# A decoder trunk on one core: heads' results turned by transposing transfers of 16-bit planes, and one stream's low parts placed behind the second normalisation

## The chip, the core and the metric

The kernel runs on one core of one Trainium2 chip. The metric is the device time of one execution in microseconds (us). Three runs of the kernel before took 1221.09, 1221.14 and 1221.6 us; the median is 1221.14 us.

The engines are named as in the profile: PE is TensorE (matrix products), PEld its weight loads, DVE is VectorE, ACT is ScalarE, POOL is GpSimd, SP is SyncE, which here only issues transfers (DMAs).

## What is computed

A trunk of two layers over 256 tokens (T) of width 1024 (D). Each layer is a feed-forward block, a mixer and a second feed-forward block, with a layer normalisation behind each:

```python
for l in range(DEPTH):                       # DEPTH = 2, T = 256, D = 1024, D_FF = 2816
    h = _swiglu(x, ffn_w1[l, 0], ffn_w3[l, 0], ffn_w2[l, 0])
    x = _layernorm(ALPHA * x + 0.5 * h, ln_g[l, 0], ln_b[l, 0])
    h = _mixer(x, ...)
    x = _layernorm(ALPHA * x + h, ln_g[l, 1], ln_b[l, 1])
    h = _swiglu(x, ffn_w1[l, 1], ffn_w3[l, 1], ffn_w2[l, 1])
    x = _layernorm(ALPHA * x + 0.5 * h, ln_g[l, 2], ln_b[l, 2])

def _mixer(x, ...):
    u, v, q, k, val, gates = split(x @ w_in)
    h_a = _chunked_sgu(gelu(u), gelu(v), ...)          # position mixing in 128-token chunks
    o = _diff_attention(rope(q), rope(k), val, lam)    # 8 heads: softmax 1 - lam * softmax 2, times val
    h_b = _rmsnorm(o, diff_ln_g) * (1 - lam_init)      # per head, over its 128 values
    m = sigmoid(gate_A) * (h_a @ w_branch[0]) + sigmoid(gate_B) * (h_b @ w_branch[1])
    return m @ w_out
```

All of it is in float32.

## The kernel before, in words

**High and low parts.** Every large product is made of three: a float32 operand is cut into a high part that PE can multiply and a low part, the rest. For weights, ACT copies the high part (`whi`, L173, 128x1024 at a time) and DVE subtracts it from the raw weight (`wlo`, L177). `stream` loads 1 MB of weights into one of four `raw` buffers (a transfer on SP's queue) and cuts it so; eight `hi` and eight `lo` buffers of half a stream each hold the parts. A load waits until the low parts of the stream four places earlier are done. Where low parts stand among DVE's other work is steered by `behind(ins)`, which makes the scheduler issue an instruction after `ins` on its engine; `after` in `stream` names such an `ins` for a stream's low parts.

**The order of PE** is written out by hand. The long gemms call `beat(w)` as they go, which moves a clock of weights forward; side tasks (generators) are resumed at the beat they asked for with `yield`, and so the matmuls of attention stand between those of the projections. The other engines' order is set by a scheduler that follows priorities and `behind`.

**The mixer** first computes `val` (`gemm_b2`), then q and k for four pairs of heads (`rope`), then gates A and B (`gemm_a2` over `wa`, eight streams), then v, u and the two branches. `attend` runs beside this, once for a pair of heads (eight times in all): scores and their exponentials (L805, L815), transposes of the probabilities by PE (L839, L844) and their copies `aT` (L841, L846), products with `val` into a side bank (L852, L854), a copy of that bank to `on` (L857), the squares for the norm (L862, written back into the bank, with sums `ss`), a reciprocal root on POOL (`rsqrt4`), the scaling of `on` (L871), four transposes of `on` by PE into another side bank (L876), and from there the high and low parts of `hb` (L881 on ACT, L882 on DVE). There are four side banks (`sbank`) in PSUM, used in turn. `hb` is read by `branch(1, hb)`, behind the gates, v and u.

**The feed-forward block** already turns its results by transfers: `front` writes the two 16-bit halves of each float32 next to each other as planes (`planes`, L678, ACT), issues a transposing transfer on SP's queue (L680), and `columns` (L664, ACT) joins the halves again.

**Where two blocks meet**, the normalisation of the first (class `Norm`) works on two halves of the tokens, t = 0 and t = 1. `finish_s` for t = 1 makes the mean (`mv`), the sum of squares on ACT (L536), a chain of small DVE instructions for the reciprocal root (`ve`, `yi`, `nwa`, `nwy`, L227 to L233), and the scaled rows (`xtok`, L539, two halves; `norm.ends[1]` is the second of them). Then PE transposes them (L608), ACT scales them (`xf`, L614), and `x` is cut into high and low parts (L217, L218). Meanwhile `gemm_b2` of the next block works on t = 0. Its streams' parts are made ahead where `norm.pre` is set, which is where a feed-forward block ends and another block follows: three places in the program. In the others of the six normalisations `norm.pre` is not set.

Of the kernel before, what the change touches and what calls it, by code (L numbers as in the profile page):

```python
# [11 lines left out]
F32 = mybir.dt.float32  # L12
# [3 lines left out]
U16 = mybir.dt.uint16  # L16
AF = mybir.ActivationFunctionType
# [3 lines left out]
P = 128  # L21
D = 1024
T = 256
NT = T // P
# [8 lines left out]
SQ = [(FB + 2 * p, FB + 2 * p + 1) for p in range(NS)]  # L33
PQ = [(k, k + 1) for k in (0, 2, *range(FB + 2 * NS, FT, 2))]
HELD = 4
HEADS = 8
HD = 64
GROUPS = 8
# [19 lines left out]
def trunk(ctx, tc, x, xT, w13a, w13b, w2s, w2p, wb, wqk, wa, wbr, wo, gateb, sgug, sgub, sguwT, sgubias, lam, diffg,  # L58
          lng, lnb, lngT, lnbT, cosT, sinT, out):
    nc = tc.nc  # L60
    V, A, G, PE = nc.vector, nc.scalar, nc.gpsimd, nc.tensor
# [9 lines left out]
    tmp = ctx.enter_context(tc.tile_pool(name="tmp", bufs=2))  # L71
# [5 lines left out]
    def name(s):  # L77
        serial[0] += 1
        return f"{s}_{serial[0]}"

    def bank():
        return psum.tile([P, 512], F32, tag="main", name=name("bank"))

    def side_bank():
        return psum.tile([P, 512], F32, tag="side", name=name("sbank"))

    def slots(s, n, dtype=F32):

        return [act.tile([P, 512], dtype, tag="slot", name=name(s)) for _ in range((n + 1) // 2)]
# [22 lines left out]
    def step():  # L112
        chunk[0] += 1
        tc.cur_priority = chunk[0] * STEP
# [12 lines left out]
    def beat(w):  # L127

        clock[0] += w
        for task in list(tasks):  # L130
            if task[0] <= clock[0]:
                turn(task)
# [15 lines left out]
    latest, added, emptied, silu, turned_by, early = [None, None], [None], [None], [None], [None], [None]  # L148

    def behind(ins):  # L150

        return tc.issue_after(ins) if ins is not None else nullcontext()

    def stream(src, width=CH, sub=HC, lent=(), after=(None, None)):

        step()
        raw = raw_pool.tile([P, CH], F32, tag="raw", name=name("raw"))
        nc.sync.dma_start(raw[:, :width], src)  # L160
        out = []
        for o in range(0, width, HC):
            if o // HC in lent:
                hi, lo = ([act.tile([P, 512], F32R, tag="slot", name=name(n)) for _ in range(2)] for n in ("lhi", "llo"))
                at = [(hi[j], lo[j]) for j in range(2)]
            else:
                hi = hi_pool.tile([P, HC], F32R, tag="hi", name=name("whi"))
                lo = lo_pool.tile([P, HC], F32R, tag="lo", name=name("wlo"))
                at = [(hi[:, p : p + sub], lo[:, p : p + sub]) for p in range(0, HC, sub)]
            for p, (h, w) in zip(range(0, HC, sub), at):  # L170
                r = raw[:, o + p : o + p + sub]
                with behind(latest[0] if o // HC in lent else early[0] or latest[0]):
                    copied = A.activation(h, r, AF.Copy)  # L173
                if o // HC in lent:
                    early[0] = copied.ins
                with behind(after[o // HC] or latest[1]):
                    V.tensor_tensor(out=w, in0=r, in1=h.bitcast(F32), op=ALU.subtract)  # L177
            out.append((hi, lo))
        return out

    def ahead(srcs):

        pre = []
        for m, n in enumerate((4, 2)):
            step()
            raw = raw_pool.tile([P, CH], F32, tag="raw", name=name("raw"))
            nc.sync.dma_start(raw, srcs[m][:, :CH])
            hi, lo = ([act.tile([P, 512], F32R, tag="slot", name=name(s)) for _ in range(n)] for s in ("lhi", "llo"))
            for j in range(n):
                with behind(early[0] or latest[0]):  # L190
                    early[0] = A.activation(hi[j], raw[:, j * 512 : (j + 1) * 512], AF.Copy).ins
            pre.append((raw, hi, lo))
        lows(pre[0], latest[1])
        return pre
# [7 lines left out]
    def rest_of(pre, after):  # L202

        (_, hi0, lo0), (raw, hi1, lo1) = pre
        lows(pre[1], after)
        hi = hi_pool.tile([P, HC], F32R, tag="hi", name=name("whi"))
        lo = lo_pool.tile([P, HC], F32R, tag="lo", name=name("wlo"))
        for p in range(0, HC, 512):
            r, h, w = (v[:, o + p : o + p + 512] for v, o in ((raw, HC), (hi, 0), (lo, 0)))
            with behind(early[0]):  # L210
                A.activation(h, r, AF.Copy)
            with behind(after):
                V.tensor_tensor(out=w, in0=r, in1=h.bitcast(F32), op=ALU.subtract)
        return [(hi0[:2], lo0[:2]), (hi0[2:], lo0[2:])], [(hi1, lo1), (hi, lo)]
# [146 lines left out]
    def gemm_b2(srcs, xh, xl, done, norm=None):  # L361

        lent, after = [()] * 4, [(None, None)] * 4
        if norm:
            lent = [(0, 1), (0,), (), ()]
            after[1:3] = [(norm.ends[0], norm.ends[0])] * 2
        ps = [[bank() for _ in range(2)] for _ in range(NT)]
        got = [[None] * 4 for _ in range(2)]  # L370
        for t in range(NT):
            for c in range(2):
                if norm:
                    norm.ready(t, c)
                    after[3] = [norm.xlo.get((0, 1))] * 2
                for m in range(2):
                    n = 2 * c + m
                    if t == 0 and n < 2 and norm and norm.pre:
                        if n == 0:
                            got[0][:2], got[1][:2] = rest_of(norm.pre, norm.ends[0])  # L380
                    elif t == 0:
                        got[m][2 * c : 2 * c + 2] = stream(srcs[m][:, c * CH : (c + 1) * CH], sub=512, lent=lent[n],
                                                           after=after[n])
                    for i in range(2 * c, 2 * c + 2):
                        rows_b(ps[t][m], t, 2 * i, got[m][i], xh, xl, KT)
            early[0] = None
            with behind(latest[0] if t == 0 else None):
                done(t, ps[t])
# [51 lines left out]
    b = side_bank()  # L440
# [5 lines left out]
    ident = const.tile([P, P], F32, name="ident")  # L446
# [180 lines left out]
    def ffn(l, f, i, norm, following=None):  # L627
# [88 lines left out]
        for n, q in enumerate(SQ):  # L716
# [3 lines left out]
            beat(1.75)  # L720
            if n < len(PQ) - HELD:
                plain_pair(n)
        u, v = s512("u"), s512("v")
        A.activation(u, S[6], AF.Copy)
        for m in range(HELD // 2):
            q = PQ[len(PQ) - HELD + 2 * m :][:2]
            held.update({(k, 0): w for k, w in zip(q, stream(w2p[l, f, len(PQ) - HELD + m]))})
        ln.more(0, 0, S[1], ALU.add, ln.scale)
        V.tensor_tensor(out=u, in0=u, in1=S[1], op=ALU.add)
        V.tensor_tensor(out=v, in0=S[5], in1=u, op=ALU.subtract)  # L730
        ln.more(0, 1, v, ALU.add, ln.scale)
        for m in range(HELD // 2):
            q = PQ[len(PQ) - HELD + 2 * m :][:2]
            held.update({(k, 1): w for k, w in zip(q, stream(w2p[l, f, len(PQ) - HELD // 2 + m]))})
# [21 lines left out]
    def mixer(l, i, norm):  # L756
# [34 lines left out]
        def attend(hp, qT, kT):  # L791
# [43 lines left out]
            b = side_bank()  # L835
# [6 lines left out]
            b = side_bank()  # L842
# [5 lines left out]
            b = side_bank()  # L848
# [7 lines left out]
            on = slots("on", 2)[0]  # L856
# [3 lines left out]
            for q in range(4):  # L860
                s = slice(q * P, (q + 1) * P)
# [3 lines left out]
                G.tensor_tensor(out=ss, in0=s2, in1=ss, op=ALU.add)  # L865
            r = rsqrt4(ss, 1.0 / (2 * HD))
            yield 2
            for q in range(4):
                s = slice(q * P, (q + 1) * P)
                with behind(emptied[0]):  # L870
                    A.activation(on[:, s], on[:, s], AF.Copy, scale=r[:, q : q + 1])  # L871
            yield 0.9
            b = side_bank()
            for j in range(2):
                for t in range(NT):
                    PE.transpose(b[:, j * T + t * P : j * T + (t + 1) * P], on[:, (t * 2 + j) * P : (t * 2 + j + 1) * P],  # L876
                                  ident)
            dl = dgs[:, l : l + 1]
            for j in range(2):
                h, s = hb[hp * 2 + j], slice(j * T, (j + 1) * T)  # L880
# [3 lines left out]

        for hp in range(HEADS // 2):
            qT = rope(wqk[l, hp, 0], HD ** -0.5)
            kT = rope(wqk[l, hp, 1], 1.0, hp == HEADS // 2 - 1)
            beside(attend(hp, qT, kT), 3.9)

        gates = []  # L890
        for br, sec in ((0, GA_), (1, GB_)):
            gt = slots("gate", KT)
            gates.append(gt)
            for c in range(KT // 2):
                (_, b), = gemm_a2([wa[l, sec, c]], both, lambda m: t512("gz"), lambda: t512("r"))
                for n in range(2):
                    s = slice(n * T, (n + 1) * T)
# [11 lines left out]
        for t in range(NT):  # L909
            mv = sm("mv", 2)  # L910
            V.bn_aggr(out=mv, in_=vst[t])
            r = rsqrt(mv[:, 1:2], EPS)
            for h in range(2):
                s = slice(h * 512, h * 512 + 512)
# [5 lines left out]
        for h in range(2):  # L920
            s = slice(h * 512, h * 512 + 512)
# [56 lines left out]
    norm = None  # L978
    for l in range(DEPTH):
        norm = ffn(l, 0, 0, norm, [wb[l, 1, m] for m in range(2)])  # L980
        norm = mixer(l, 1, norm)
        norm = ffn(l, 1, 2, norm, [w13b[l + 1, 0, m, 0] for m in range(2)] if l < DEPTH - 1 else None)
# [92 lines left out]
```

## Time and profile before

| | |
|---|---|
| median of three runs | 1221.14 us |
| profiled execution | 1220.97 us |
| its span, first to last instruction | 1219.3 us |
| PE busy | 1210.0 us (99%) |
| DVE busy | 948.8 us (78%) |
| ACT busy | 820.0 us (67%) |
| mean granted clock of PE | 1.000 |

The rows of a timeline give the start in us from the span's start, the time from the first start to the last end of the merged instructions, engine, line, operation, output and inputs, and how many there are; in brackets stands the engine's idle time ahead of it and what ended it. Instructions on one engine overlap at their ends, so what one costs its engine is read from start to start.

### The profile page before, as it was taken

The numbers are of one execution on the slowest core, as the hardware profiler recorded it, in microseconds if no ns is written. First come the engines' busy times: TensorE is split into PE (matmuls) and PEld (weight loads), VectorE is DVE, ScalarE is ACT, GpSimd is POOL, SyncE is SP. The second block draws the span as 40 slices with busy tenths as digits, with TensorE's granted clock in tenths as the row PEclk, the third lists the DMA queues.
The fourth block names the chain that finished last, engine by engine and source line by source line (L and its number), as shares of the span: only waits on it lengthen the run. The fifth ranks groups of instructions, "written<-read, shape, count | busy, mean of one in ns | idle before, by whom it ended". The sixth has DMA issues, their size and how long they took to land.

```text
span 1219.3 us, 16603 instructions
## 1 busy us (share of the span) xinstructions
PE 1210.0 (99%) x6033; PEld 1018.2 (84%) x6033; DVE 948.8 (78%) x1540; ACT 820.0 (67%) x1340; POOL 87.7 (7%) x184
## 2 busy tenths in 40 slices
PE   9999999999999999999999999999999999999998
PEld 8888888888888888888878888888888888888886
DVE  6658998886587985579985679979856879747797
ACT  7677676689665575775766776666786655667761
POOL 0100000244100000000000000002430000000000
PEclk9999999999999999999999999999999999999999
DMA  8976666654644667665667655656546456576551
GB/s 319 334 246 178 218 226 214 214 169 165 249 171 167 216 176 264 192 202 210 218 218 252 194 176 205 255 215 202 165 175 232 173 172 243 177 238 209 181 202 48
DMA packets 82339, 252.29 MB, mean 207 GB/s; under 512 B 47520, under 2 KB 48592, under 8 KB 55632
## 3 DMA queue, kind: packets, MB, share of 16 engines
q1 hardware_dynamic: 78288, 238.31, 58.1%
q0 software_dynamic: 3536, 12.13, 3.1%
q8 instruction: 47, 0.77, 0.2%
q10 hardware_dynamic: 432, 0.79, 0.2%
q14 instruction: 36, 0.29, 0.1%
HBM read 235.47 MB, written 1.05 MB: 194 GB/s over the span
## 4 chain that ended last, share of the span: by engine, by line
PE 97%; DVE 1%; ACT 1%; DMA 0%; issue 0%; DVEq 0%; ACTq 0%
PE bank L255 36%; PE sbank L255 26%; PE bank L267 17%; PE bank L274 9%; PE sbank L267 2%; PE bank L430 2%; PE sbank L274 1%; PE sbank L805 1%; PE sbank L608 1%; DVE wlo L177 1%; PE sbank L854 1%; PE sbank L935 1%; ACT xf L614 0%; ACT sq L536 0%; PE sbank L852 0%; PE sbank L876 0%
## 5 line engine op out<-in xcount | busy, mean ns | idle before, releaser
L177 DVE TENSOR_TENSOR wlo<-raw,whi 128x1024 fp32r<-128x1024 f32 (+1 forms) x396 | 437.8, 1122 | 158.9 <-ACT whi L173 118.7
L173 ACT ACTIVATE whi<-raw 128x1024 fp32r<-128x1024 f32 (+1 forms) x396 | 375.5, 972 | 163.8 <-PE bank L255 61.7
L255 PE MATMUL bank<-whi,x 128*128 128x512 f32 x840 | 264.6, 390 | 0.0
L255 PEld LDWEIGHTS bank<-whi,x 128*128 128x128 f32 x840 | 157.7, 188 | 32.5
L255 PE MATMUL bank<-wlo,x 128*128 128x512 f32 x420 | 163.5, 389 | 0.0
L255 PE MATMUL sbank<-whi,x 128*128 128x512 f32 x512 | 159.0, 389 | 0.0
L267 PE MATMUL bank<-x,whi 128*128 128x512 f32 x640 | 158.3, 395 | 0.0
L267 PEld LDWEIGHTS bank<-x,whi 128*128 128x128 f32 x640 | 116.5, 188 | 25.9 <-issue 2.6
L255 PEld LDWEIGHTS sbank<-whi,x 128*128 128x128 f32 x512 | 96.1, 188 | 20.0
L337 ACT ACTIVATE shi<-raw 128x1024 fp32r<-128x1024 f32 (+1 forms) x80 | 73.4, 946 | 51.7 <-DVE raw L352 26.4
L255 PE MATMUL sbank<-wlo,x 128*128 128x512 f32 x256 | 99.6, 389 | 0.0
L339 DVE TENSOR_TENSOR slo<-raw,shi 128x1024 fp32r<-128x1024 f32 (+1 forms) x80 | 85.3, 1088 | 14.1 <-ACT shi L337 13.1
L255 PEld LDWEIGHTS bank<-wlo,x 128*128 128x128 f32 x420 | 78.9, 188 | 16.0
L274 PE MATMUL bank<-x,wlo 128*128 128x256 f32 x640 | 85.9, 285 | 0.0
L274 PEld LDWEIGHTS bank<-x,wlo 128*128 128x128 f32 x640 | 81.6, 191 | 2.3
L275 ACT ACTIVATE r<-bank 128x256 f32<-128x256 f32 x112 | 41.9, 379 | 27.6 <-PE bank L274 27.6
L614 ACT ACTIVATE xf<-sbank,ln_b,ln_g 128x128 f32<-128x128 f32 x80 | 30.0, 455 | 42.1 <-PE sbank L608 42.1
L255 PE MATMUL sbank<-whi,hhi 128*128 128x512 f32 x144 | 56.4, 391 | 0.0
L255 PEld LDWEIGHTS sbank<-wlo,x 128*128 128x128 f32 x256 | 48.0, 188 | 9.9
L255 PE MATMUL sbank<-wlo,hhi 128*128 128x512 f32 x144 | 56.1, 389 | 0.0
L255 PE MATMUL sbank<-whi,hlo 128*128 128x512 f32 x144 | 56.1, 389 | 0.0
L490 POOL DMA_DIRECT2D bc<-in_lng x6 | 3.2, 532 | 711.2 <-DVE bc L489 711.2
(246 smaller groups left out, 1984.6 us busy)
## 6 DMA issues: line engine op xcount, KB each, us to landing
raw<-in_w13b SPq DMA_DIRECT2D x76, 1024.0 KB, 5.3
raw<-in_w2p SPq DMA_DIRECT2D x24, 1024.0 KB, 4.8
raw<-in_wa SPq DMA_DIRECT2D x24, 1024.0 KB, 5.3
raw<-in_w2s SPq DMA_DIRECT2D x20, 1024.0 KB, 4.8
raw<-in_wb SPq DMA_DIRECT2D x16, 1024.0 KB, 5.2
raw<-in_wqk SPq DMA_DIRECT2D x16, 1024.0 KB, 5.0
raw<-in_wbr SPq DMA_DIRECT2D x16, 1024.0 KB, 4.8
raw<-in_w13a SPq DMA_DIRECT2D x8, 1024.0 KB, 4.8
```

What stands on the lines that cost most here:

```text
L173: copied = A.activation(h, r, AF.Copy)
L177: V.tensor_tensor(out=w, in0=r, in1=h.bitcast(F32), op=ALU.subtract)
L255: PE.matmul(ps, xx, w, start=start and n == 0, stop=stop and n == 2)
L267: PE.matmul(b[-1], hi[:, k * P : (k + 1) * P], xc(k), start=k == 0, stop=False)
L274: PE.matmul(b[n][:, :T], lo[:, k * P : (k + 1) * P], xc(k)[:, :T], start=False, stop=k == KT - 1)
L275: emptied[0] = A.activation(r[:, s], b[n][:, T:], AF.Copy, scale=scale).ins
L337: A.activation(h, r, AF.Copy)
L339: V.tensor_tensor(out=w, in0=r, in1=h.bitcast(F32), op=ALU.subtract)
L430: PE.matmul(ps[t][m], x[:, j, o + t * P : o + (t + 1) * P], y, start=k0 + j == 0 and o == 0 and y is hi, stop=k0 + j == KT - 1 and y is lo)
L608: PE.transpose(b[:, k * P : (k + 1) * P], self.y[t][:, h * 512 + k * P : h * 512 + (k + 1) * P], ident)
L614: A.activation(xf[:, s], b[:, s], AF.Identity, scale=self.gT[:, f], bias=self.bT[:, f])
L805: PE.matmul(banks[m][:, j * nk : (j + 1) * nk], rows(qT, m, j, t * P, P), rows(kT, m, j, 0, nk), start=True, stop=True)
```

## The change

1. In `attend`, the four scalings no longer write `on` in place but `os`, the first half of a tile `both` of which there is one buffer. ACT makes planes of it in the second half of the tile (`planes`), a transposing transfer on SP's queue turns them into `tt`, and after `yield LAND` (5 on the clock of weights) ACT joins the halves into `turned` in SBUF (`join`). The four transposes on PE and their side bank are gone; L881 and L882 read `turned`.
2. In `gemm_b2`, the low parts of the last of the four streams are tied behind `norm.ends[1]`, the end of the second normalisation, where `norm.pre` is set. Before, they were tied behind `norm.xlo[0, 1]`, the low part of `x` of t = 0.

```diff
+LAND = 5
...
+    def planes(pk, src):
+        A.activation(pk.rearrange("p (w k) -> p w k", w=2), src.bitcast(U16).rearrange("p (k w) -> p w k", w=2), AF.Copy)
+
+    def turning(pk, n):
+        tt = slots("tt", 2)[0][:, : n * P].bitcast(U16)
+        nc.sync.dma_start_transpose(out=tt.rearrange("p (c t) -> p c t", c=2 * n), in_=pk)
+        return tt
+
+    def join(dst, tt):
+        with behind(emptied[0]):
+            A.activation(dst.bitcast(U16).rearrange("p (k w) -> p k w", w=2), tt.rearrange("p (w k) -> p k w", w=2), AF.Copy)
...
-                    after[3] = [norm.xlo.get((0, 1))] * 2
+                    after[3] = [norm.ends[1] if norm.pre else norm.xlo.get((0, 1))] * 2
...
+            both_ = tmp.tile([P, 2, 512], F32, tag="columns", name=name("both"), bufs=1)
+            os, pk = both_[:, 0], both_[:, 1].bitcast(U16)
             for q in range(4):
-                s = slice(q * P, (q + 1) * P)
+                t, j = q // 2, q % 2
                 with behind(emptied[0]):
-                    A.activation(on[:, s], on[:, s], AF.Copy, scale=r[:, q : q + 1])
-            yield 0.9
-            b = side_bank()
-            for j in range(2):
-                for t in range(NT):
-                    PE.transpose(b[:, j * T + t * P : j * T + (t + 1) * P], on[:, (t * 2 + j) * P : (t * 2 + j + 1) * P],
-                                  ident)
+                    A.activation(os[:, j * T + t * P : j * T + (t + 1) * P], on[:, q * P : (q + 1) * P], AF.Copy,
+                                 scale=r[:, q : q + 1])
+            planes(pk, os)
+            tt = turning(pk, 4)
+            yield LAND
+            b = slots("turned", 2)[0]
+            join(b, tt)
```

The order of the built programs shows what moved. On DVE, at the second normalisation ahead of the first mixer (`wlo_1817` and `wlo_1823` are the low parts of the last stream, `xtok_144` the scaled rows of t = 1), before:

```order
L233 TENSOR_SCALAR nwy_1725<-nwa_1724,yi_1721 128x1
L177 TENSOR_TENSOR wlo_1817<-raw_1814,whi_1816 128x512
L232 TENSOR_SCALAR nwa_1728<-nwy_1725,ve_1720 128x1
L177 TENSOR_TENSOR wlo_1817<-raw_1814,whi_1816 128x512
L233 TENSOR_SCALAR nwy_1729<-nwa_1728,nwy_1725 128x1
L177 TENSOR_TENSOR wlo_1823<-raw_1814,whi_1822 128x512
L232 TENSOR_SCALAR nwa_1732<-nwy_1729,ve_1720 128x1
L177 TENSOR_TENSOR wlo_1823<-raw_1814,whi_1822 128x512
L233 TENSOR_SCALAR nwy_1733<-nwa_1732,nwy_1729 128x1
L539 TENSOR_SCALAR xtok_144<-xtok_144,mv_1715,nwy_1733 128x512 x2
```

and after:

```order
L249 TENSOR_SCALAR nwy_1725<-nwa_1724,yi_1721 128x1
L248 TENSOR_SCALAR nwa_1728<-nwy_1725,ve_1720 128x1
L249 TENSOR_SCALAR nwy_1729<-nwa_1728,nwy_1725 128x1
L248 TENSOR_SCALAR nwa_1732<-nwy_1729,ve_1720 128x1
L249 TENSOR_SCALAR nwy_1733<-nwa_1732,nwy_1729 128x1
L555 TENSOR_SCALAR xtok_144<-xtok_144,mv_1715,nwy_1733 128x512 x2
L178 TENSOR_TENSOR wlo_1817<-raw_1814,whi_1816 128x512 x2
L178 TENSOR_TENSOR wlo_1823<-raw_1814,whi_1822 128x512 x2
```

The four low parts stood one by one between the small instructions of the root and now stand behind the scaled rows, so that the root's chain runs on unbroken. The same holds at the two other places. (Line numbers of the program after are larger, since lines were added: its L178 is L177 before, L248 and L249 are L232 and L233, L555 is L539.)

On ACT, in the first layer, where the first pair's results are scaled and the second pair's bank is copied and squared (`on_2412` is the first pair's result, `sbank_2625` or `sbank_2629` the second pair's bank, `hb` the parts that branch B reads), before:

```order
L871 ACTIVATE on_2412<-on_2412,nwy_2510 128x128 x4
L857 ACTIVATE on_2632<-sbank_2625 128x512
L275 ACTIVATE r_2609<-bank_2599 128x256
L862 ACTIVATE sbank_2625,ss_2634<-sbank_2625 128x128
L898 ACTIVATE gate_2554<-gz_2610,gbh 128x256
L862 ACTIVATE sbank_2625,ss_2634<-sbank_2625 128x128 x2
L898 ACTIVATE gate_2554<-gz_2610,gbh 128x256
L862 ACTIVATE sbank_2625,ss_2634<-sbank_2625 128x128
L881 ACTIVATE hb_1906<-sbank_2672,dgs 128x256
L173 ACTIVATE whi_3037<-raw_3035 128x1024
L881 ACTIVATE hb_1907<-sbank_2672,dgs 128x256
L173 ACTIVATE whi_3041<-raw_3035 128x1024
```

and after:

```order
L889 ACTIVATE both_2621<-on_2412,nwy_2510 128x128 x4
L184 ACTIVATE both_2621<-both_2621 128x1024
L291 ACTIVATE r_2609<-bank_2599 128x256
L873 ACTIVATE on_2636<-sbank_2629 128x512
L916 ACTIVATE gate_2554<-gz_2610,gbh 128x256
L878 ACTIVATE sbank_2629,ss_2638<-sbank_2629 128x128
L174 ACTIVATE whi_3037<-raw_3035 128x1024
L878 ACTIVATE sbank_2629,ss_2638<-sbank_2629 128x128
L916 ACTIVATE gate_2554<-gz_2610,gbh 128x256
L878 ACTIVATE sbank_2629,ss_2638<-sbank_2629 128x128
L174 ACTIVATE whi_3041<-raw_3035 128x1024
L878 ACTIVATE sbank_2629,ss_2638<-sbank_2629 128x128
```

L889, L184, L873 and L878 are the scaling, the planes, the bank's copy and its squares in the program after. The planes of `both_2621` come in ahead of the second `r` and the copy of the bank; the two `hb` copies are gone from here (they now come a pair later, behind a join), and the fourth square of the bank now stands behind both weight copies.

On SP's queue, from the load of the last gate stream on (`in_wb` are v's streams, the following `in_wa` u's), before:

```order
L160 DMA raw_3175<-in_wa 128x2048
L160 DMA raw_3242<-in_wb 128x2048
L160 DMA raw_3276<-in_wb 128x2048
L160 DMA raw_3316<-in_wb 128x2048
L160 DMA raw_3350<-in_wb 128x2048
L160 DMA raw_3457<-in_wa 128x2048
L160 DMA raw_3508<-in_wa 128x2048
```

and after:

```order
L161 DMA raw_3176<-in_wa 128x2048
L189 DMA_TRANSPOSE tt_2627<-both_2621 128x8x128
L161 DMA raw_3240<-in_wb 128x2048
L161 DMA raw_3274<-in_wb 128x2048
L189 DMA_TRANSPOSE tt_2832<-both_2826 128x8x128
L161 DMA raw_3320<-in_wb 128x2048
L161 DMA raw_3354<-in_wb 128x2048
L189 DMA_TRANSPOSE tt_3005<-both_2999 128x8x128
L161 DMA raw_3461<-in_wa 128x2048
L161 DMA raw_3512<-in_wa 128x2048
```

Three of the first layer's four transposing transfers stand here between the weight loads, each ahead of loads that came in an unbroken row before; the fourth follows behind u's third load. PE's own order loses the eight groups of transposes and is otherwise the same; POOL's is unchanged.

## The prediction

> **What bounds the kernel now.** I read the page first: busy shares, the granted clock, and the chain of work that ended last.
>
> ```profile
> span 1219.3 us, 16603 instructions
> PE 1210.0 (99%) x6033; PEld 1018.2 (84%) x6033; DVE 948.8 (78%) x1540; ACT 820.0 (67%) x1340; POOL 87.7 (7%) x184
> PEclk9999999999999999999999999999999999999999
> PE 97%; DVE 1%; ACT 1%; DMA 0%; issue 0%; DVEq 0%; ACTq 0%
> ```
>
> PE is the bound from end to end at full clock, so only two kinds of edit pay: one that takes instructions out of PE's queue, or one that ends a wait of PE. PE's list of waits has one that repeats, the transposes L608 behind the second normalisation, three times:
>
> ```profile
> PE sbank L608 <- DVE xtok L539: 2.9, 3, 1.0
> ```
>
> **Part 1, PE's transposes removed.** A busy PE overlaps itself, so I read the price from starts in the timeline: a gate stream without transposes, and one with them in its middle (last pair, first layer).
>
> ```profile
> 302.56 3.82 PE L267 MATMUL bank<-x,whi 128*128 128x512 f32 x16
> 306.22 2.08 PE L274 MATMUL bank<-x,wlo 128*128 128x256 f32 x16
> 308.13 2.00 PE L267 MATMUL bank<-x,whi 128*128 128x512 f32 x8
> 309.97 0.60 PE L876 MATMUL sbank<-ident,on 128*128 128x128 f32 x4
> 310.33 2.11 PE L267 MATMUL bank<-x,whi 128*128 128x512 f32 x8
> 312.27 2.06 PE L274 MATMUL bank<-x,wlo 128*128 128x256 f32 x16
> ```
>
> Sixteen products take 306.22 - 302.56 = 3.66 us; the same sixteen with the four transposes take 312.27 - 308.13 = 4.14. A group costs 0.48 us (not the 0.60 of its row), eight groups 3.8 us, all on the path: **-3.8**.
>
> **Part 2, the low parts moved.** Around L608, first of the three places; the first three rows are the undisturbed pattern earlier in the same stage:
>
> ```profile
> 177.41 0.39 PE L255 MATMUL sbank<-whi,hlo 128*128 128x512 f32 x1
> 177.64 0.60 PE L608 MATMUL sbank<-ident,xtok 128*128 128x128 f32 x4
> 178.00 0.48 PE L255 MATMUL sbank<-whi,hhi 128*128 128x512 f32 x1
> 189.28 0.39 PE L255 MATMUL bank<-whi,x 128*128 128x512 f32 x1
> 190.65 0.66 PE L608 MATMUL sbank<-ident,xtok 128*128 128x128 f32 x4 [0.98 <-DVE xtok L539]
> 191.06 0.48 PE L255 MATMUL bank<-whi,x 128*128 128x512 f32 x1
> ```
>
> From the last product before to the first behind: 178.00 - 177.41 = 0.59 undisturbed, 191.06 - 189.28 = 1.78 with the wait. The wait costs 1.19 us, more than the 0.98 in brackets. What DVE did meanwhile:
>
> ```profile
> 186.79 0.21 DVE L233 TENSOR_SCALAR nwy<-nwa,yi 128x1 f32<-128x1 f32 x1
> 186.91 0.68 DVE L177 TENSOR_TENSOR wlo<-raw,whi 128x512 fp32r<-128x512 f32 x1
> 187.51 0.27 DVE L232 TENSOR_SCALAR nwa<-nwy,ve 128x1 f32<-128x1 f32 x1
> 189.20 0.68 DVE L177 TENSOR_TENSOR wlo<-raw,whi 128x512 fp32r<-128x512 f32 x1
> 189.80 0.21 DVE L233 TENSOR_SCALAR nwy<-nwa,nwy 128x1 f32<-128x1 f32 x1
> 190.04 1.00 DVE L539 TENSOR_SCALAR xtok<-xtok,mv,nwy 128x512 f32<-128x512 f32 x2
> ```
>
> Each of the four low parts holds the chain for 187.51 - 186.91 = 0.60. Without them the chain from 186.79 is four small instructions (0.21 + 0.27 + 0.21 + 0.27, some 0.03 between), so the last `nwy` starts near 187.9 and, with the 190.65 - 189.80 = 0.85 from there to L608, PE could go on at 188.7. It wants to at 189.28 + 0.23 = 189.5: 0.8 us to spare, the wait is gone. What is late next? The low parts. Scaled rows from about 188.1 to 189.1, then four times 0.60: the first is ready near 189.8, the fourth near 191.6. PE comes back from L608 at 189.9, has six products of the stream before (0.23 each), and reads the first of these low parts near 191.5, the fourth behind the next transposes, past 193. No new wait. ACT's `xf` and DVE's `x` of t = 1 hang on L608 and come earlier with it; the one raw buffer comes free some 1.7 us later than at 189.9, for a load whose weights PE multiplies streams later. I take the whole wait, three times: **-3.6**; the ends are 0 (the chain ends in another wait) and -3.6.
>
> **Part 1's price on ACT.** Planes and join are shapes that the feed-forward block has (grouped view), and the window from the first to the last pair is ACT's fullest (windows view: PE, PEld, DVE, ACT busy):
>
> ```profile
> L664 ACT ACTIVATE columns<-turned 128x1024 uint16<-128x1024 uint16 x40 | 44.9, 1170 | 0.0
> L678 ACT ACTIVATE planes<-silu 128x1024 uint16<-128x1024 uint16 x40 | 42.0, 1053 | 5.8 <-DVE silu L677 4.6
> 266.00:286.00 20.00, 20.00 (x130) 17.10 (x129) 15.95 (x41) 18.22 (x58) 5.96 (x16) 1.00 0.41 144
> 286.00:306.00 20.00, 20.00 (x124) 17.74 (x123) 11.67 (x18) 17.76 (x46) 10.87 (x32) 1.00 0.47 158
> ```
>
> Eight pairs times 1.05 + 1.17 = 17.8 us of ACT, 8.9 in each layer. In these 40 us ACT is idle for 1.78 + 2.24 = 4.0: it will be full, and something comes late. What may: weight copies are made up to eight half streams ahead of PE and may slip by several us; the gates' `r` must be done one stream (5.57 us) later. Tight is only what shares side banks. With one side bank less in the round, the scores of the fourth pair (L805) now write the bank that the second pair's squares (L862) just left; before, two banks stood between. The rows from there:
>
> ```profile
> 266.46 0.36 ACT L275 ACTIVATE r<-bank 128x256 f32<-128x256 f32 x1
> 266.73 1.27 ACT L871 ACTIVATE on<-on,nwy 128x128 f32<-128x128 f32 x4
> 267.90 0.58 ACT L857 ACTIVATE on<-sbank 128x512 f32<-128x512 f32 x1
> 268.38 0.36 ACT L275 ACTIVATE r<-bank 128x256 f32<-128x256 f32 x1
> 268.64 0.26 ACT L862 ACTIVATE sbank<-sbank 128x128 f32<-128x128 f32 x1
> 268.83 0.19 ACT L862 ACTIVATION_READ_ACCUMULATOR sbank<-sbank 128x1 f32 x1
> 269.36 0.51 ACT L898 ACTIVATE gate<-gz,gbh 128x256 f32<-128x256 f32 x1 [0.34 <-DVE gz L277]
> 271.44 0.18 ACT L862 ACTIVATION_READ_ACCUMULATOR sbank<-sbank 128x1 f32 x1
> 271.88 1.05 ACT L173 ACTIVATE whi<-raw 128x1024 fp32r<-128x1024 f32 x1
> 273.93 1.13 PE L805 MATMUL sbank<-qk,qk 64*128 64x256 f32 x8
> ```
>
> Before, the squares end at 271.6, PE writes at 273.9. I lay the new order along these starts. From 266.46: r 0.27, four scalings 1.17, planes 0.96, r 0.27, bank's copy 0.48, gate 0.42: 270.0. Square 0.28, weight copy 0.95, square 0.28: 271.5. The second gate waits for DVE, which has two low parts (1.13 each) between the `gz` halves from 268.9: about 271.9. Gate 0.42, square 0.28, copy 0.95, square with its read 0.38: 273.9. PE, 0.48 earlier by its own saving, reaches the second bank at 273.93 - 0.48 + 0.14 = 273.6. A wait of 0.35 us, in each layer once: **+0.7**. Ends: 0 (ACT 0.35 faster than laid) and +1.4 (each 0.7). For the later pairs I find no such place: the two weight copies that stood ahead of the third pair's `aT` go behind it and make room for planes and join, and the last pairs' banks are not wanted again until position mixing.
>
> **What costs nothing, and its cover.** `hb` is complete later, by a pair: the last near 319 by the same laying, against 315 before, and PE reads it first here:
>
> ```profile
> 359.98 3.82 PE L267 MATMUL bank<-hb,whi 128*128 128x512 f32 x16
> turned<-planes SPq DMA_TRANSPOSE x40, 3.9
> L680 SPq DMA_TRANSPOSE turned<-planes x40: 1233/1268/2827, 26.6 to 1146.0; - x40
> ```
>
> So 40 us cover transfers that land in 3.9 us; if that cover were gone each would cost up to 3.9. On SP's queue each holds 1.27 us and, should its planes be late, the loads behind it: v's and u's streams. Those wait for low parts of four streams earlier anyway and may slip by some 2 us; their data lie ready long before ACT copies them. On the other side, ACT's scaling of a pair waits until the pair before has left `both`; planes to next scaling is 11 us or more, transfer 3.9.
>
> **The sum.** 1220.97 (the profiled execution; span 1219.3) - 3.8 - 3.6 + 0.7 = 1214.3; the median stands 0.17 higher, so 1214.4 us, 0.55% less. By the ends of these terms: 1213.8 to 1218.7. (About 0.2%, 2.4 us, is what a measurement of this kernel can tell from no change.)
>
> The Trainium skill has a rule against the change: "VectorE: DVE Perf Modes", section "The three transpose paths", gives a 128x128 transpose in bf16 as 390 ns on TensorE and 1309 ns by DMA, and its rules for authors prefer TensorE where PSUM will do as the destination. By its figures, as an estimate, eight blocks of 16 bits in a pair take 10.5 us by transfer. The rows answer it: a transfer of this size lands in 3.9 us, and PE's share of 0.48 is what is on the path here.
>
> **Rivals.**
> - ACT overfull, and slower in the end. 2.0 us of ACT more between a pair's scaling and the next pair's `aT` and exponentials; if PE's transposes and products with `val` are late by all of it for three pairs in two layers, that is +12 us: 1225.6. Against it: the two copies moved out of that stretch (1.9 us) and PE's list of waits, which has none there now. It turns to slower than before when the mean wait in a pair exceeds 7.4 / 8 = 0.9 us. Partly, it gives 1218 to 1222. Chance 0.11: 0.06 slower, 0.05 within 0.2%.
> - The transfers show: PE, or ACT ahead of it, waits for each of eight landings, 8 x 3.9 = 31 us: 1245. The rule above would have it so. 40 us of cover speak against it. Chance 0.02.
> - Part 2 does not do what it says: the sum of squares on ACT or the small chain ends as late, and L608 waits on. 1214.4 + 3.6 = 1218.0. Against it: the rows' 0.8 us to spare. Chance 0.06, still faster.
>
> **How the numbers follow.** The forecast has 0.81: 1213.4 to 1216.5 with the side bank's wait at its ends and some small waits that I did not see. With the third rival that makes faster 0.86 (0.81 + 0.06, less 0.01 for the tail), same 0.06, slower 0.08. The range leaves out the overfull ACT and the transfers, and reaches to part 2 failing: 1212.9 to 1218.0.
>
> **What would show it.** No L876 among PE's rows; L608's wait gone from PE's list, 0.59 around it; a wait of some 0.35 of the fourth pair's L805 for ACT, once in a layer; planes and joins of about 1.1 us, and ACT above 95% between the first and the third pair; `hb` ready 30 us ahead of its reader. Wrong would be the prediction if PE waited for `aT`, for probabilities, or for low parts behind L608.

## The result and the profile after

The changed kernel takes 1215.17 us (median of four runs, 1215.01 to 1215.4), the kernel before 1221.2 beside it: ratio 0.9949, 95% interval 0.9936 to 0.9963. That is 6.0 us less; 6.7 was forecast (1214.4 after 1221.1, range 1212.9 to 1218.0). The profiled execution took 1215.40 us.

The page of the changed kernel, its first rows and the chain by engine:

```profile
span 1213.7 us, 16560 instructions
PE 1207.2 (99%) x6001; PEld 1016.2 (84%) x6001; DVE 950.4 (78%) x1540; ACT 833.1 (69%) x1356; POOL 91.0 (8%) x184
PEclk9999999999999999999999999999999999999999
PE 97%; DVE 1%; POOL 1%; DMA 0%; ACT 0%; issue 0%; SPq 0%; DVEq 0%; POOLq 0%; ACTq 0%
```

PE is still the bound at full clock. Its busy time alone fell by only 2.8 us, so the gain has to be looked for in the starts of its instructions. PE's whole list of waits:

```profile
PE sbank L458 <- DVE warm L454: 1.0, 1, 1.0
PE sbank L592 <- DVE xtok L571: 1.0, 1, 1.0
PE bank L446 <- ACT whi L233: 0.2, 1, 0.2
PE sbank L596 <- ACT minus L594: 0.2, 1, 0.2
```

The three waits at the transposes behind the second normalisation (now L624) are gone. What this list does not show is a wait inside a merged group; that one comes below. I set PE's starts of the two kernels side by side, instruction for instruction. The difference (after minus before) moves at these places:

| place | step, us | forecast |
|---|---|---|
| first products | +0.54 | - |
| L624, three places | -1.15, -1.19, -1.15 = -3.49 | -3.6 |
| groups of transposes gone | 8 x (-0.46 to -0.49) = -3.80 | -3.8 |
| fourth pair's scores L821, first and second layer | +0.53, +0.78 = +1.31 | +0.7 |
| all else | -0.11 | 0 |
| at the end | -5.55 | -6.7 |

The three rows that the change explains (L624, transposes, scores) give -5.98 together, the medians -6.03. The first row lies at the landing of the first weights, where no instruction moved. In the profiled executions of the experiments below it lies between -0.2 and +0.6.

**The transposes.** The gate streams of the last pair in the first layer, where L876 stood:

```profile
301.03 3.82 PE L283 MATMUL bank<-x,whi 128*128 128x512 f32 x16
304.68 2.08 PE L290 MATMUL bank<-x,wlo 128*128 128x256 f32 x16
306.60 3.82 PE L283 MATMUL bank<-x,whi 128*128 128x512 f32 x16
310.25 2.08 PE L290 MATMUL bank<-x,wlo 128*128 128x256 f32 x16
```

Both streams now take 3.65 us for sixteen products (310.25 - 306.60), as the undisturbed one did.

**The second normalisation**, first place, DVE and then PE:

```profile
188.43 0.21 DVE L249 TENSOR_SCALAR nwy<-nwa,nwy 128x1 f32<-128x1 f32 x1
188.68 1.00 DVE L555 TENSOR_SCALAR xtok<-xtok,mv,nwy 128x512 f32<-128x512 f32 x2
189.60 2.49 DVE L178 TENSOR_TENSOR wlo<-raw,whi 128x512 fp32r<-128x512 f32 x4
189.82 0.39 PE L271 MATMUL bank<-whi,x 128*128 128x512 f32 x1
190.05 0.60 PE L624 MATMUL sbank<-ident,xtok 128*128 128x128 f32 x4
190.40 0.49 PE L271 MATMUL bank<-whi,x 128*128 128x512 f32 x1
```

From the last product to the first behind it is 190.40 - 189.82 = 0.58, the undisturbed pattern. The chain's last instruction starts at 188.43; with 0.85 from there PE could have gone on at 189.28, so 0.77 us are to spare (0.8 was forecast). The four low parts run behind, to 192.1, and no product waits for them.

**The fourth pair's scores**, in the first and the second layer:

```profile
272.83 1.70 PE L821 MATMUL sbank<-qk,qk 64*128 64x256 f32 x8
274.46 2.11 PE L283 MATMUL bank<-x,whi 128*128 128x512 f32 x8
873.36 1.95 PE L821 MATMUL sbank<-qk,qk 64*128 64x256 f32 x8
875.25 2.11 PE L283 MATMUL bank<-x,whi 128*128 128x512 f32 x8
```

Eight scores and the step to the next product took 1.07 us before; now 1.63 and 1.89. ACT's timeline in the first layer, cut to six rows; the last is the end of the squares that the scores wait for:

```profile
265.83 0.36 ACT L291 ACTIVATE r<-bank 128x256 f32<-128x256 f32 x1
267.39 1.06 ACT L184 ACTIVATE both<-both 128x1024 uint16<-128x1024 uint16 x1
269.78 1.06 ACT L174 ACTIVATE whi<-raw 128x1024 fp32r<-128x1024 f32 x1
271.33 0.51 ACT L916 ACTIVATE gate<-gz,gbh 128x256 f32<-128x256 f32 x1 [0.21 <-DVE gz L293]
272.03 1.04 ACT L174 ACTIVATE whi<-raw 128x1024 fp32r<-128x1024 f32 x1
273.18 0.18 ACT L878 ACTIVATION_READ_ACCUMULATOR sbank<-sbank 128x1 f32 x1
```

From the gates' `r` to the end of the last square is 273.36 - 265.83 = 7.53 us (forecast: 266.46 to 273.9, 7.44). The scores fill two banks, and only the second of them waits. In the kernel before the first scores of the two banks start side by side, at 273.93 and 273.96, and so do the three pairs behind them; so here PE wants the second bank at 272.83 + 0.03 = 272.86. Its first score into it starts at 273.41, 0.05 us behind the end of the squares, while two scores of the first bank run ahead alone. How full ACT is (fourth busy time) shows in two windows:

```profile
266.00:286.00 20.00, 20.00 (x120) 16.73 (x119) 15.16 (x40) 18.65 (x56) 4.38 (x16) 1.00 0.43 143
286.00:306.00 20.00, 20.00 (x127) 18.05 (x126) 10.30 (x16) 19.34 (x48) 8.65 (x24) 1.00 0.65 184
```

That is 93% and 97%, up from 91% and 89%. The transfers land in 2.8 us (median), but for the last of each layer, 7.2 and 6.9 us:

```profile
L189 SPq DMA_TRANSPOSE tt<-both x8: 1243/1257/1340, 268.5 to 913.9; - x8
DMA to landing us min/median/max: 2.7/2.8/7.2
```

### The profile page after: what moved, and what is told of

It is laid out like the page before. It is cut to its first block, busy times and chain, and to the rows that moved or that the text cites. A ratio compares the mean times of both kernels' runs of the same rounds, so it can differ in the third digit from the quotient of the medians.

```text
span 1213.7 us, 16560 instructions
## 1 busy us (share of the span) xinstructions
PE 1207.2 (99%) x6001; PEld 1016.2 (84%) x6001; DVE 950.4 (78%) x1540; ACT 833.1 (69%) x1356; POOL 91.0 (8%) x184
## 3 DMA queue, kind: packets, MB, share of 16 engines
HBM read 235.47 MB, written 1.05 MB: 195 GB/s over the span
## 4 chain that ended last, share of the span: by engine, by line
PE 97%; DVE 1%; POOL 1%; DMA 0%; ACT 0%; issue 0%; SPq 0%; DVEq 0%; POOLq 0%; ACTq 0%
PE bank L271 38%; PE sbank L271 26%; PE bank L283 16%; PE bank L290 8%; PE sbank L283 2%; PE bank L446 2%; PE sbank L290 1%; PE sbank L821 1%; PE sbank L624 1%; PE sbank L953 1%; PE sbank L870 0%; DMA xraw<-in_xT 0%; DVE wlo L178 0%; PE sbank L868 0%; PE sbank L855 0%
## 5 line engine op out<-in xcount | busy, mean ns | idle before, releaser
L178 DVE TENSOR_TENSOR wlo<-raw,whi 128x1024 fp32r<-128x1024 f32 (+1 forms) x396 | 436.5, 1123 | 150.5 <-ACT whi L174 117.1
```

## The experiments

All were timed in five rounds against the kernel before on the same chip. Steps are differences of PE's starts, as above.

**The two halves alone.** Low parts alone is the kernel before with the one line of `gemm_b2`; transposes alone is the changed kernel without it:

```diff
-                    after[3] = [norm.ends[1] if norm.pre else norm.xlo.get((0, 1))] * 2
+                    after[3] = [norm.xlo.get((0, 1))] * 2
```

Expected of the low parts alone: 

> Only the low parts are moved; TensorE's transposes of the heads' results stay. Theory: the sum is additive, this half is three waits at the transposes of the normalised rows, 1.14 us each by the starts in the profile after: 1221.2 - 3.4 = 1217.8 us, no wait of the xtok transposes for DVE, nothing new behind them. Rival: the moved low parts come late for the products behind the transposes, and part of the gain is lost there: 1218.5 to 1220.

Expected of the transposes alone: 

> Only the transposes go to transfers; the low parts stay ahead of the second normalisation. Theory: eight groups at 0.49 us are saved, the fourth pair's scores wait 0.56 us in the first layer and 0.83 in the second for ACT's squares in the side bank: 1221.2 - 3.9 + 1.4 = 1218.7 us, and the three waits of 1.0 us at the xtok transposes stay. Rival: the two halves meddle with each other (ACT's or DVE's queue), and the halves alone give together at least 0.5 us more or less than the 6.0 of both.

Low parts alone: 1217.76 against 1221.15, ratio 0.9974 (0.9965 to 0.9984), 3.4 less. Transposes alone: 1218.52, ratio 0.9979 (0.9971 to 0.9988), 2.6 less, and the wait at L624 stands in its list with 2.9 us, three times, while the scores wait 0.53 and 0.72. Together 6.0: the halves add up. (In the low parts alone, where PE comes 3.4 us earlier, the scores of the second layer wait 0.25 us as well.)

**Half of the low parts.** Two of the four stand ahead of the normalisation again; nothing else moves on any engine:

```diff
-                    after[3] = [norm.ends[1] if norm.pre else norm.xlo.get((0, 1))] * 2
+                    after[3] = [norm.ends[1] if norm.pre and m else norm.xlo.get((0, 1)) for m in range(2)]
```

> As the changed kernel, but two of the four low parts stand ahead of the second normalisation again (in its chain of small instructions), two behind; nothing else moves. Theory: each part holds the chain for 0.60 us, and the changed kernel has 0.77 us to spare at the transposes (last small instruction at 188.43, + 0.85 = 189.28, TensorE is there at 190.05). Two parts give a wait of 2 x 0.60 - 0.77 = 0.43, three times: 1215.2 + 1.3 = 1216.5 us. Rival one: the wait goes by halves, 3 x 0.57 = 1.7: 1216.9 us. Rival two: all four parts were needed to make it wait, 1215.2 us.

1215.9 us (ratio 0.9955, 0.9943 to 0.9968), 0.7 above the changed kernel. DVE and PE, first place:

```profile
189.40 0.21 DVE L249 TENSOR_SCALAR nwy<-nwa,nwy 128x1 f32<-128x1 f32 x1
190.25 0.66 PE L624 MATMUL sbank<-ident,xtok 128*128 128x128 f32 x4
```

The two parts hold the chain not for 1.20 but for 189.40 - 188.43 = 0.97 us, since each also fills time in which the next small instruction would wait for the one before: without parts the four steps to the last one take 188.43 - 187.32 = 1.11 us, 0.28 each. 0.97 - 0.77 = 0.20, and PE's starts step by 0.21 to 0.23 at each place, half of the 0.43 that was expected. So a spare time is used up first, and only what exceeds it is paid; the price by halves (rival one, 0.57 at each place) and no price (rival two) are both excluded by these steps.

**Is it the lateness of ACT's squares?** Three edits leave the arithmetic of the changed kernel as it is. First, squares taken from the copy in SBUF:

```diff
+            sq = s512("sq").bitcast(BF16)
...
-                A.activation(b[:, s], b[:, s], AF.Square, accum_out=ss[:, q : q + 1])
+                A.activation(sq[:, s], on[:, s], AF.Square, accum_out=ss[:, q : q + 1])
```

> As the changed kernel, but ACT takes the squares of a pair from the copy in SBUF and not from the side bank, so that the bank is free as soon as it is copied; ACT has as many instructions as before. Theory: the fourth pair's scores no longer wait, 0.56 + 0.83 = 1.4 us come back: 1215.2 - 1.4 = 1213.8 us; the scores take 1.07 from their first start to the next product in both layers. Rival: ACT is overfull there and what is late is not tied to the bank: the wait stays or moves to the next reader of ACT's results, 1215.2 us.

1216.55 us (ratio 0.9965, 0.9951 to 0.9979): 1.4 slower than the changed kernel and not faster. POOL, DVE and PE in the first layer:

```profile
267.75 1.29 POOL L797 TENSOR_TENSOR swap<-swap,sin_t 128x512 f32<-128x512 f32 x1
269.08 0.69 DVE L801 TENSOR_TENSOR qk<-qk,swap 128x512 f32<-128x512 f32 x1 [3.26 <-POOL swap L797]
270.22 0.83 PE L855 MATMUL sbank<-ident,pp 128*128 128x128 f32 x4 [0.39 <-DVE pp L840]
273.30 1.14 PE L821 MATMUL sbank<-qk,qk 64*128 64x256 f32 x8
```

The scores no longer wait (1.14). But the scheduler laid the queues anew: on SP the four transfers of a rotation went behind the next weight load. POOL's rotation is 2.7 us later than in the changed kernel, DVE stands for it, and the transposes of the probabilities behind it wait for DVE. This run does not price the squares, since it moved another thing as well.

Second, planes issued later:

```diff
+            yield 1.5
             planes(pk, os)
             tt = turning(pk, 4)
-            yield LAND
+            yield LAND - 1.5
```

> As the changed kernel, but a pair's planes are issued later, behind at least two of the next pair's squares; the weight copies that stood between the squares go behind them too, so that ACT reaches the fourth square some 1.5 us earlier. Theory: lateness of ACT's squares is the whole price of 1.4 us, and it goes: 1213.8 us, scores at 1.07 in both layers. Rival: with ACT full, what is put behind the squares (planes, transfers, weight copies) makes another instruction late, as in the kernel with squares from SBUF, and the gain is lost: 1215 to 1216.5 us with a new wait of PE.

1213.4 us (ratio 0.9936, 0.9923 to 0.9948). PE in both layers, and the end of ACT's squares in the first:

```profile
271.12 0.18 ACT L878 ACTIVATION_READ_ACCUMULATOR sbank<-sbank 128x1 f32 x1
272.68 1.13 PE L821 MATMUL sbank<-qk,qk 64*128 64x256 f32 x8
872.67 1.14 PE L821 MATMUL sbank<-qk,qk 64*128 64x256 f32 x8
873.74 2.14 PE L283 MATMUL bank<-x,whi 128*128 128x512 f32 x8
```

The squares end 1.4 us ahead of PE, the scores take 1.07, and PE's starts step against the changed kernel at these two places alone, -0.54 and -0.79, though the scheduler moved rows of ACT, DVE and SP elsewhere too. This is the price of +1.31, given back. In ACT's queue the planes (269.29) still stand ahead of the last two squares; what now stands behind the last one are both weight copies (271.20 and 272.89, 1.9 us together). So it is mainly their place that the edit changed. Since the 1.8 us between the medians came from two chips, both kernels ran once more side by side:

> The changed kernel as it is, as the measure for the kernel with the later planes on the same chip. Its first products waited 0.17 us for a weight copy and its second group came 0.54 us later than in the kernel before, in the one profiled execution; in other kernels with the same beginning this lies between -0.2 and +0.5. Theory: that is scatter of the first landings, the time is 1215.2 us, and the rows of the fourth pair's scores stay at 0.53 and 0.78 of waiting. Rival: the late start belongs to the changed kernel, and is 0.5 again.

> The kernel with the planes issued 1.5 units later, once more, beside the changed kernel. Theory: it is faster by the two waits of the fourth pair's scores, 0.53 + 0.78 = 1.3 us, 1213.9 us beside 1215.2. Rival: the 1.8 us between them were chips and landings, and they are alike within 0.3 us.

1215.1 us (1214.64 to 1215.49; ratio 0.995, 0.9937 to 0.9962) and 1213.41 us (1213.21 to 1213.95; ratio 0.9938, 0.9924 to 0.9951). The later planes are 1.7 us faster with no overlap of the runs: -0.54 and -0.67 at the scores, -0.40 at the first products. These began 0.59 late in the changed kernel once more, and 0.19 late in the other; whether a part of that belongs to the changed kernel stays open. The kernel with later planes beats both.

Third, planes and joins on POOL (the two copies as `G.tensor_copy` in place of `A.activation`):

> As the changed kernel, but planes and joins are copied by POOL in place of ACT (17.8 us less on ACT). Theory: ACT's squares come 1 us or more earlier and the fourth pair's scores no longer wait: 1213.8 us. Rival one: POOL takes so long for 128x1024 of 16 bits (its rotation of 128x512 floats takes 1.3) that what stands behind on its queue is late, the next pair's rotation or its reciprocal roots: 1216 to 1220 us. Rival two: the order of ACT's queue decides and not its load, and the wait stays: 1215.2 us.

1216.32 us (ratio 0.9962, 0.9949 to 0.9976). PE's wait, from its list:

```profile
PE sbank L821 <- ACT sbank L878: 1.6, 2, 0.9
```

POOL, the third of DVE's four instructions on the probabilities, and ACT in the first layer:

```profile
267.05 1.32 POOL L184 COPY both<-both 128x1024 uint16<-128x1024 uint16 x1 [1.09 <-ACT both L889]
267.39 1.13 DVE L840 SCALAR_TENSOR_TENSOR pp<-pp,c,pp 128x128 f32<-128x128 f32 x1
269.15 0.51 ACT L916 ACTIVATE gate<-gz,gbh 128x256 f32<-128x256 f32 x1 [1.42 <-DVE gz L293]
```

The same instruction of DVE in the changed kernel, without a copy on POOL:

```profile
267.76 0.34 DVE L840 SCALAR_TENSOR_TENSOR pp<-pp,c,pp 128x128 f32<-128x128 f32 x1
```

The scores wait longer, though ACT's busy time is 14.0 us less (819.0). In ACT's queue the squares still stand behind the two gates, and the last one behind both weight copies. The gates wait for `gz`, which DVE makes behind the probabilities: ACT stands 1.42 us at the first gate and 0.67 at the second. DVE's four instructions take 2.18 instead of 1.40 us while POOL copies, all of it in the third, and the squares end at 273.9. Without that 0.79 us they would end near 273.1, an estimate from these rows, still 0.7 behind the 272.4 at which PE begins the scores. So rival two, the order of the queue, keeps the wait, and DVE's delay adds to it, which neither rival had. The time lies in rival one's range, but not for its reason: POOL's rotation and roots are in time.

**Place or amount?** Doubled planes, and in another kernel doubled joins (`planes(pk, os)` or `join(b, tt)` written twice):

> As the changed kernel, with each pair's planes written twice, 8 x 0.96 us of ACT more, ahead of the next pair's squares. Theory: only the fourth pair's scores feel it, once in a layer, by one planes each: 2 x 0.96 = 1.9 us, 1217.1 us. Rival one: ACT is overfull as a whole between the first and the third pair, and three pairs in two layers are late: 6 x 0.96 = 5.8 us, 1221 us. Rival two: the late squares are not what PE waits for: 1215.2 us.

> As the changed kernel, with each join written twice, 8 x 1.1 us of ACT more, as much as the doubled planes took, but at other places: the first join stands in ACT's queue behind the second pair's squares. Theory: the place in the queue decides; the fourth pair's scores wait as in the changed kernel (0.56 and 0.83) and nothing else does: 1215.2 us. Rival: the amount decides, as much as with the doubled planes: 1215.2 + 3.9 = 1219.1 us.

Doubled planes: 1219.13 us (ratio 0.9984, 0.9975 to 0.9993), 4.0 above the changed kernel; doubled joins: 1219.57 (0.9988, 0.9979 to 0.9997), 4.4 above. My theory failed in both; the doubled joins cost what their rival had (1219.1). With doubled planes PE's list has:

```profile
PE bank L283 <- DVE gz L293: 2.2, 2, 1.1
PE sbank L868 <- ACT aT L862: 0.7, 2, 0.3
```

With doubled joins:

```profile
PE sbank L954 <- DVE vg L936: 2.6, 2, 1.6
PE bank L271 <- DVE gz L293: 1.0, 2, 0.5
```

With doubled planes the scores wait less than in the changed kernel (0.25 us in the first layer; the scheduler dropped the weight copies from between the squares), but products with `val`, gate banks and position mixing wait. With doubled joins the scores indeed stay as they were, and PE is late by 0.8 us in each layer at a bank behind the gates and by 1.3 and 1.8 us at position mixing, L954. Position mixing hangs on v's normalisation, which has little to spare in the changed kernel (DVE, then PE):

```profile
346.60 1.41 DVE L935 SCALAR_TENSOR_TENSOR vg<-vg,nwy,bc 128x512 f32<-128x512 f32 x2
348.71 1.05 PE L953 MATMUL sbank<-wsT,vg 128*128 128x128 f32 x8
```

The last rows of `vg` end at 348.01, 0.70 us ahead of PE's first product there; in the kernel before it was 0.86. The engine without time to spare is DVE here, not ACT: from 326 to 348 us DVE is 99% busy in the changed kernel (84% before) and ACT 66%. With doubled joins ACT's last result of v starts only 0.4 us later than in the changed kernel (334.53 and 334.15). But ACT's weight copies were late before it, DVE made their low parts late, and DVE's statistics of that result start 3.1 us later (changed kernel, then doubled joins):

```profile
335.96 0.69 DVE L924 BATCH_NORM_STATS2 vst<-vg 128x6 f32<-128x512 f32 x1
339.05 0.68 DVE L925 BATCH_NORM_STATS2 vst<-vg 128x6 f32<-128x512 f32 x1
```

So what is added to ACT's queue comes out at the next reader with a short chain, at position mixing by way of DVE's queue.

**Transfers.** Joins issued right behind the transfers (`LAND = 1`), and each pair's planes turned by two transfers (`turning(pk, 4)` twice, the join reading the second):

> As the changed kernel, but the joins are issued 4 units earlier, right behind the planes and their transfer, so that there is little time for the transfer to land. Theory: the join stands ahead of the last square in place of a weight copy (1.17 for 0.95 us, and some 0.3 of waiting for the landing): the fourth pair's scores wait 0.5 us more in each layer, 1215.2 + 1.0 = 1216.2 us. Rival: the cover between planes and join is what hides eight landings of 2.8 us, ACT stands for them and PE behind it: 1215.2 + 22 = 1237 us at most, over 1220 if a third of it shows.

> As the changed kernel, with each pair's planes turned by two transfers of the same size, the join reading the second: 1.27 us of SP's queue and one more landing of 2.8 us ahead of each join. Theory: transfers are covered, the time is that of the changed kernel but for what the new order of ACT's queue does to the second pair's squares, between -1.4 us (they come in time) and +0.5: 1213.8 to 1215.7 us. Rival: transfers or SP's queue are at their limit, and four or more landings show: 1226 us or more.

`LAND = 1`: 1217.01 us (ratio 0.9965, 0.9952 to 0.9977), 1.8 above the changed kernel, with runs from 1215.8 to 1219.0. Two transfers: 1219.36 (0.9985, 0.9976 to 0.9994), 4.2 above, with runs from 1217.7 to 1220.8, outside both expectations. At the scores, where I had looked for the price, PE's starts step by 0.14 and 0.28 us with `LAND = 1` (0.5 in each layer was expected) and by 0.57 and 0.22 with two transfers. The larger part is elsewhere. With `LAND = 1`, PE's wait and the last pair's join on ACT, first layer:

```profile
PE sbank L953 <- DVE vg L935: 1.4, 1, 1.4
```

```profile
322.38 1.18 ACT L195 ACTIVATE turned<-tt 128x1024 uint16<-128x1024 uint16 x1 [6.15 <-DMA tt<-both]
```

The same join with two transfers:

```profile
322.25 1.18 ACT L195 ACTIVATE turned<-tt 128x1024 uint16<-128x1024 uint16 x1 [2.69 <-DMA tt<-both]
```

The last pair's transfer is issued at 313.0 (with `LAND = 1`), lands 9.3 us later, and its join can start only at 322.4. ACT stands for it for 6.15 us with v's results behind it in its queue, and position mixing pays: 1.69 us in the first layer with `LAND = 1`, 1.65 and 1.82 with two transfers. The cover that `LAND` gives is needed for ACT's sake in the last pair, not for `hb`.

Just ahead of that transfer POOL issues four transfers of 256 KB for position mixing (310.8 to 312.4 us), and the last of them lands at 319.9. In all traces each of these transposing transfers that took over 4 us was issued while others were under way, and landed 0.8 to 2.6 us behind the last of those. In the last pair these are POOL's four, with and without a load of weights; with doubled planes a load of weights alone does it to the second pair (5.4 and 7.5 us). With the copies on POOL the four are issued behind the last pair's transfer, and all eight are quick:

```profile
DMA to landing us min/median/max: 2.7/2.7/2.8
```

So the late landing goes with what is under way ahead of it. No run changes that alone, and what holds the transfer up stays open.

## Why the prediction held, and where it was off

- **Transposes on PE, -3.8**: measured -3.80. Starts gave the right price (0.48), the row's 0.60 would have given 4.8.
- **Low parts, -3.6**: -3.49 in the trace and -3.4 when done alone. The spare time of 0.8 was 0.77. Too high was the hold of 0.60 for each part: two took 0.97 together, and by the rows before, four took 189.80 - 186.79 = 3.01 less the 1.11 without parts, 1.90. And 1.90 - 0.77 = 1.13 is the wait that went (1.15 to 1.19), while four times 0.60 less 0.8 is 1.6, which the prediction could have seen not to fit its own 1.19.
- **The side bank, +0.7**: the term that was mis-sized; +1.31. ACT's rows were laid to 0.1 us (7.53 against 7.44). The second bank's first score was laid 0.14 behind the first bank's, an eighth of the 1.07 for eight scores; but the scores run in pairs, one for each bank, and it is 0.03. ACT's hand-over, 0.05 us, was not counted. That makes 7.53 - 7.00 - 0.03 + 0.05 = 0.55 in the first layer, where PE's starts step by 0.53. The scores of the first bank that run ahead save nothing, since from the second bank's first score to the next product it is 274.46 - 273.41 = 1.05 us, what all eight take without a wait (1.07). In the second layer ACT came later still beside PE (`r` 6.76 us ahead of PE's scores, 7.00 in the first), and I had taken the layers as equal. The upper end of +1.4 held it.
- **The reason given for that wait was wrong in part.** I wrote that the scores now write the squares' bank because one bank less is in the round. In the built programs the same scores wait for the same squares in both kernels, at the first of their two banks before and at the second after. What changed is that planes and two weight copies stand ahead of the last square; with the planes issued later the weight copies went behind the squares, and the wait was gone with the same banks.
- **"For the later pairs I find no such place"**: right, but with 0.70 us to spare at position mixing, where I had not looked. Four experiments paid there.
- **Cover of the transfers**: `hb` is complete at 324.5, not 319, since the last pair's transfer is issued late (313.1) and takes 7 us to land; PE reads it first at 357.98, 33 us later. No landing shows in PE's time, but ACT stands 1.34 us for the last landing in the first layer and 1.06 in the second, which the 40 us of cover did not consider. The Trainium skill, "VectorE: DVE Perf Modes", section "The three transpose paths", has 1309 ns for one 128x128 block by transfer; here eight blocks of 16 bits land together in 2.8 us (median), so its figure doesn't scale with the blocks.
- **The rivals**: ACT overfull was the nearest to the truth. It came true in small, at two places, and to the size that the prediction calls partly (1218 to 1222) as soon as 1 us per pair was added (1219.1 to 1219.6). Of the signs, ACT above 95% was met in one of the two windows (93% and 97%). Transfers that show and a part 2 that does nothing did not occur.

## What to carry to other kernels

Price an instruction on the bounding engine by starts around it, and a wait by the spare time that its chain has, since only the excess is paid. When work moves to an engine that is nearly full, find every reader of that engine with a short chain, however far behind and by way of other engines too: the added time comes out at the first that has no spare time. Then try to issue the new work later: here 1.5 units on the program's clock gave back what the scores had cost, since the scheduler then put two weight copies behind the squares.

## What was not expected of the hardware

In this trace a DVE instruction with two inputs in SBUF that begins while POOL copies within SBUF ends only behind the copy. Of the four instructions on the probabilities, the first two (0.48 us each) began ahead of POOL's copy and took as long as without it. The third began inside it, at 267.39, and ended at 268.52, 0.15 us behind the copy's end: 1.13 us instead of 0.34, and 1.12 in the second layer. `gz`, which reads one input from SBUF and one from PSUM, took its usual 0.41 us inside POOL's copies. The Trainium skill, "SBUF — State Buffer", section "Who interferes with whom", says that a DVE instruction with two SBUF inputs contends with a GpSimd instruction that reads SBUF; the trace agrees. A copy moved to an idle POOL was therefore not free, since DVE's chain was the one that ACT waited for.
